# First stage of a hybrid HGRN2/Hyena layer: modulation and transposes before the filter kernels' blocks, all four v units in one stage, small tables on another queue

## The chip, the cores and the metric

The kernel runs on one core of one Trainium2 chip. A core has five engines with an instruction stream each, which they work off strictly in order: TensorE (PE, matmuls and transposes; its weight loads are listed as PEld), VectorE (DVE), ScalarE (ACT), GpSimd (POOL) and SyncE (SP, which here issues most transfers). An engine waits on semaphores of the others; work that stands behind a waiting instruction on the same engine waits with it. The metric is the device time of one execution in microseconds; less is better.

## The reference

One layer of a flow-matching backbone in float32: 128 context tokens and 512 sample tokens (T = 640) of width 1024. Cut to what matters for the change:

```python
# modulation of the tokens by a condition (context tokens by c_ctx, sample tokens by c)
mod = silu(c) @ ada_w + ada_b                 # six parts of 1024
h = x * (1 + scale) + shift                   # parts 0 and 1
z = h @ w_in                                  # 5 HGRN, 3 Hyena, 2 gate parts
# HGRN2, in both directions, 8 heads of 128
v = heads(i_raw)                              # a part of z
fg = lb + (1 - lb) * sigmoid(f_raw); k = 1 - fg
# chunks of 32 tokens, b = cumsum(log fg):
q_in = q * exp(b); k_in = k * exp(-b); k_st = k * exp(b_last - b)
# Hyena: filters from a small network
hf = sin(freq[0] * (z_pos @ w1 + b1))
hf = sin(freq[1] * (hf @ w2 + b2))
hf = sin(freq[2] * (hf @ w3 + b3))
filt = (hf @ w4) * window                     # then a long convolution through its spectrum
```

After both mixers come gates, an output projection, a layer norm, a SwiGLU feed-forward block and a second norm.

## The kernel before

Matrix products in float32 are made of three passes: each operand is split into a rounded high part and a low part (hi/lo, names with h and l), and high x high, high x low and low x high are summed. A split takes a cast (ScalarE or VectorE) and a subtraction (VectorE or POOL).

The kernel runs in stages: the first stage, up to 115.6 us of the profile; M1 (the large projections, a Winograd-like scheme); the Hyena convolution with its projection; HGRN; and the output and feed-forward stages. The changed parts lie in the first stage, and in HGRN's beginning. The first stage does:

- the filter network (L495 to L508): matmuls f1, f2 and f3, each followed by a sine layer of four VectorE operations (L479 to L483) and a Sin on ScalarE; its result is split into `hf_hi` and `hf_lo`;
- the tables `kt` (`ktab`, L512): three loads, each with a cast to `kth` and a difference `ktl` on POOL;
- the tokens `x`: five loads of 512 KB (`x_load`, L450), transposed by TensorE into `xT` (`x_transpose`, L457), ten groups of four transposes;
- the modulation: for each of four blocks `nb` of 512 columns two loads of 1 MB (`ada_load`, L397), eight matmuls in two quads (`ada_quad`, L406), a copy `md` on ScalarE (L417), four transposes `adaT` (L430) and additions on VectorE into `modT`. The loads' buffers are three (`araw`);
- `make_h` (L459 on), for each of eight blocks `k`: two modulation operations, a cast to `hTh` and a difference `hTl`. Tables of letters say which engine does which: `HMOD` for the modulation, `HSUB` for the difference (S ScalarE, V VectorE, G POOL);
- the filter kernels, for each of four channel blocks `cc`: `kern_load` (w4 and win), `kern_a` (the weights `wsd`, `whi`, `whl`; ten matmuls `ks`; five windows `af` with two buffers; their splits `abh` and `abl`), `kern_b` (6 matmuls `kp` and 48 matmuls `k`, then sums into `ko`) and a store to `kd`;
- v units (L696): a product of all tokens with 256 columns, 120 matmuls each, with weights that are loaded as `raw` and split into `wh` and `wl`. v0 and v1 are made here, v2 and v3 in the HGRN stage, after head 0's gate g0;
- the block operands of M1 (step `e`).

The order is a string of steps, `PLAN`, read from left to right: `x0` is a load, `T0` its transposes, `L0`, `A0`, `B0`, `W0` the parts of filter block 0, `k0` a table, `D0` the two loads of modulation block 0 and `M0` its quads, copy and transposes, `h0` a `make_h`, `V0` a v unit, `p`, `t`, `q` the parameters. The instructions of a step are handed to a scheduler, which keeps the order of each buffer and places work on each engine by dependency and by order in the string; `tc.high_priority()` moves work ahead. Steps such as `M0` and the splits of weights have that priority before the change. The HGRN stage has a string of its own, `HGSEQ`: for head 0 `a0 b0 q0 g0` are projections, `e0` the element chain of exponentials and products on ScalarE and VectorE (`t`, `ff`, `gg`, `xx`; `hg_elem`, L1157 on), and `s0` begins with TensorE's transposes `kT` (L1233) of one of its results, `t6`.

The stream of weights looks ahead by the table `LOOK`, and `HIE` and `WSUB` say by which engine each weight tile is cast and subtracted. Both are read by the tile's number.

Of the kernel before, what the change touches and what calls it, by code (L numbers as in the profile page):

```python
# [162 lines left out]
def body(tc, I, O):  # L163
# [16 lines left out]
    def tt(out, a, b, op, eng=None):  # L180
        return (eng or V).tensor_tensor(out=out, in0=a, in1=b, op=op)  # L181

# [123 lines left out]
    def params_T():  # L306
        ps = tr_bank("pr3_ps")
        PE.transpose(ps[:, 0:65], prow2, ident[0:65, 0:65])
        V.tensor_copy(cT.rearrange("p a k -> p (a k)"), ps[:, 49:65])
# [90 lines left out]
    def ada_quad(nb, i):  # L400
        raw = ada["raw"].pop((nb, i))
        if i == 0:
            ada["ps"][nb] = mm_bank(f"ada{nb}")
        ps = ada["ps"][nb]
        for g in range(4):
            PE.matmul(ps[32 * g:32 * g + 32, :], scT[:, 4 * i + g, :], raw[:, g, :], start=i == 0, stop=i == 1)  # L406
# [70 lines left out]
    def sin_layer(psrc, i, nm):  # L477
# [5 lines left out]
        V.tensor_scalar(a, a, HALF, -HALF, ALU.min, ALU.max)  # L483
        act(a, a, AF.Sin, scale=-TWO_PI)
# [7 lines left out]
    def filter_mlp():  # L492
# [10 lines left out]
        for hf in range(2):  # L503
            ps = sc_bank(f"f3_{hf}")
            rs = slice(hf * ORD, hf * ORD + ORD)
            PE.matmul(ps[:, 0:HT], w3[rs].rearrange("p a n -> p (a n)"), h2[rs], start=True, stop=True)
# [5 lines left out]
    def ktab(i):  # L512
# [3 lines left out]
        cpy("k", i, kth[:, cs], raw)  # L516
# [42 lines left out]
    def kern_b(cc, ab):  # L559
        c0 = cc * 256  # L560
        kth_ = (kth, ktl)
        def kout(n, nm):
# [4 lines left out]
            return t
# [6 lines left out]
        t = kout(1, "p")  # L574
        cpy("o", 3 * cc, t[:, 0], pk.rearrange("p (x n) -> p x n", x=2))
        out = [(t, 4, 1)]
        for kt in range(2):
# [12 lines left out]
            t = kout(2, kt)  # L590
# [8 lines left out]

    def order_after(ins, prev):  # L600
        if prev is not None:
            tc.add_manual_dep(
                ins.ins, prev.ins.name,
                mybir.DependencyInfo(mybir.DependencyClass.NoSync, mybir.DependencyReason.DATA),
                reason="issue order")
# [112 lines left out]
    v_add(0)  # L718
    v_add(1)
# [3 lines left out]
    def start():  # L723
        stream["stop"] = 4
# [1061 lines left out]
```

## Time and profile before

| quantity | value |
|---|---|
| runs | 1427.77, 1429.8 and 1691.48 us |
| median of the runs | 1429.8 us |
| the profiled execution's own time | 1430.8 us |
| its span on the core | 1428.1 us |

A row of the timeline has the start and the busy time in us, engine, line, operation, the tile written and those read, partitions x elements, a count (xcount) and in brackets the idle time of the engine before it with what ended it. The page's slices are tenths of busy time over 40 equal parts of the span of 35.7 us each; the first stage is the first three and a bit:

```profile
PE   4989999999999999999999999998999999999997
DVE  6886786647889734568778875578876766766427
ACT  3655554433323212455565673337444434442121
POOL 4230000020000000000000000000000000000003
DMA  7944665674333374422232224632343233357211
```

The waits of the queue that issues the loads, up to 110 us (waited for: us in total, times, longest):

```profile
SPq L526 <- DVE af L181: 18.3, 2, 9.2
SPq L450 <- PE xT L457: 6.1, 1, 6.1
SPq L397 <- PE ada L406: 4.6, 2, 2.5
```

A load of `win` waits until the windows before it are used up, a load of `x` or of the modulation until its buffer is free; all loads behind it in SP's queue wait with it.

### The profile page before, as it was taken

The numbers are of one execution on the slowest core, as the hardware profiler recorded it, in microseconds if no ns is written. First come the engines' busy times: TensorE is split into PE (matmuls) and PEld (weight loads), VectorE is DVE, ScalarE is ACT, GpSimd is POOL, SyncE is SP. The second block draws the span as 40 slices with busy tenths as digits, with TensorE's granted clock in tenths as the row PEclk, the third lists the DMA queues.
The fourth block names the chain that finished last, engine by engine and source line by source line (L and its number), as shares of the span: only waits on it lengthen the run. The fifth ranks groups of instructions, "written<-read, shape, count | busy, mean of one in ns | idle before, by whom it ended". The sixth has DMA issues, their size and how long they took to land. (4 is left out here: it accounts for less than half of the span.)

```text
span 1428.1 us, 23421 instructions
## 1 busy us (share of the span) xinstructions
PE 1377.5 (96%) x9513; PEld 1291.3 (90%) x9513; DVE 990.8 (69%) x1751; ACT 619.4 (43%) x1011; POOL 63.4 (4%) x56
## 2 busy tenths in 40 slices
PE   4989999999999999999999999998999999999997
PEld 2689889999999999999999999988999998998886
DVE  6886786647889734568778875578876766766427
ACT  3655554433323212455565673337444434442121
POOL 4230000020000000000000000000000000000003
PEclk9999999999999999999999999999999999999999
DMA  7944665674333374422232224632343233357211
GB/s 244 332 138 144 214 215 175 206 249 152 91 97 107 107 231 146 140 85 80 76 95 62 67 67 139 223 118 77 97 124 115 89 108 97 94 193 279 74 60 74
DMA packets 198855, 195.63 MB, mean 137 GB/s; under 512 B 7581, under 2 KB 155773, under 8 KB 197980
## 3 DMA queue, kind: packets, MB, share of 16 engines
q1 hardware_dynamic: 194860, 179.75, 40.0%
q0 software_dynamic: 2160, 9.15, 1.7%
q10 hardware_dynamic: 1728, 5.24, 0.9%
q8 instruction: 74, 1.21, 0.3%
q14 instruction: 33, 0.27, 0.1%
HBM read 162.91 MB, written 31.21 MB: 136 GB/s over the span
## 5 line engine op out<-in xcount | busy, mean ns | idle before, releaser
L181 DVE TENSOR_TENSOR wl<-raw,wh 128x1024 fp32r<-128x1024 f32 x96 | 117.2, 1223 | 134.1 <-ACT wh L357 133.4
L357 ACT CAST wh<-raw 128x1024 fp32r<-128x1024 f32 x90 | 94.1, 1049 | 221.1 <-PE pb L611 41.0
L1424 PE MATMUL fo<-wh,act 128*128 128x512 f32 (+1 forms) x440 | 130.6, 380 | 0.0
L1424 PEld LDWEIGHTS fo<-wh,act 128*128 128x128 f32 x440 | 81.2, 188 | 15.9
L1424 PE MATMUL fo<-wl,act 128*128 128x512 f32 (+1 forms) x220 | 83.4, 379 | 0.0
L611 PE MATMUL hy<-hTh,wh 128*128 128x320 f32 x256 | 79.6, 311 | 0.0
L611 PE MATMUL hy<-hTh,wl 128*128 128x320 f32 x256 | 79.1, 309 | 0.0
L611 PE MATMUL hy<-hTl,wh 128*128 128x320 f32 x256 | 79.1, 309 | 0.0
L611 PE MATMUL f<-hTh,wh 128*128 128x320 f32 x224 | 70.7, 316 | 0.0
L611 PE MATMUL f<-hTl,wh 128*128 128x320 f32 x224 | 69.6, 311 | 0.0
L611 PE MATMUL f<-hTh,wl 128*128 128x320 f32 x224 | 69.2, 309 | 0.0
L181 POOL TENSOR_TENSOR y<-y,gb 128x512 f32<-128x512 f32 x8 | 11.6, 1453 | 905.8 <-ACT y L170 905.5
L1424 PEld LDWEIGHTS fo<-wl,act 128*128 128x128 f32 x220 | 41.3, 188 | 7.9
L611 PEld LDWEIGHTS hy<-hTh,wh 128*128 128x128 f32 x256 | 48.1, 188 | 0.0
L611 PEld LDWEIGHTS hy<-hTl,wh 128*128 128x128 f32 x256 | 48.1, 188 | 0.0
L611 PEld LDWEIGHTS hy<-hTh,wl 128*128 128x128 f32 x256 | 48.0, 188 | 0.0
L170 ACT ACT_TABLE_LOAD x36 | 46.2, 1283 | 1.4 <-PEq L1770 0.7
L708 PE MATMUL v<-wh,hTl 128*128 128x256 f32 x160 | 45.1, 284 | 1.4 <-POOL hTl L181 1.4
L708 PE MATMUL v<-wl,hTh 128*128 128x256 f32 x160 | 44.8, 284 | 1.6 <-DVE wl L181 1.6
L708 PE MATMUL v<-wh,hTh 128*128 128x256 f32 x160 | 44.6, 283 | 0.0
L611 PEld LDWEIGHTS f<-hTl,wh 128*128 128x128 f32 x224 | 42.2, 188 | 0.0
L611 PEld LDWEIGHTS f<-hTh,wh 128*128 128x128 f32 x224 | 42.1, 188 | 0.0
(2291 smaller groups left out, 4699.1 us busy)
## 6 DMA issues: line engine op xcount, KB each, us to landing
raw<-in_w_in SPq DMA_DIRECT2D x52, 512.0 KB, 3.9
rf<-in_ffn_w_in SPq DMA_DIRECT2D x42, 512.0 KB, 4.9
araw<-in_ada_w SPq DMA_DIRECT2D x20, 1024.0 KB, 6.1
rm<-in_w_in SPq DMA_DIRECT2D x28, 512.0 KB, 4.8
raw<-in_ffn_w_out SPq DMA_DIRECT2D x22, 512.0 KB, 4.9
sd<-my SPq DMA_DIRECT2D x28, 320.0 KB, 2.3
kk<-kd SPq DMA_DIRECT2D x20, 256.0 KB, 2.6
ad<-y SPq DMA_DIRECT2D x16, 320.0 KB, 4.0
```

The lines of the kernel that those rows point to most:

```text
L170: r = S.activation(out, in_, func, bias=bias, scale=scale)
L181: return (eng or V).tensor_tensor(out=out, in0=a, in1=b, op=op)
L357: (V.tensor_copy if HIE[i] == "V" else S.copy)(hi, raw)
L611: r = PE.matmul(ps[:, 0:HT], w[a][:, k, :], x[b][:, k, c0:c0 + HT], start=k == 0 and i == 0, stop=k == kt - 1 and i == 2)
L708: PE.matmul(ps[:, (t - t0) * 256:(t - t0) * 256 + 256], hT[b][:, k, t * P:t * P + P], w[a][:, k % 4, :], start=k == 0 and i == 0, stop=k = ...
L1424: PE.matmul(ps, x(t, b, k0 + kk), w[a][:, kk, :], start=first and kk == 0 and i == 0, stop=last and kk == nk - 1 and i == 2)
```

## The change

`PLAN` is written anew up to M1's first steps, and some work changes its engine, buffer or queue. Before:

```text
x0 k0 L0 k1 x4 k2 p mlp t L1 T0 x3 T4 A0 x2 D0 T2 A1 x1 L2 B0 M0 T1 D2 A2 M2 T3 h0 L3 B1 D1 A3 h1 B2 M1 D3 h2 h3 M3 h4 W2 W0 h5 h6 h7 W1 q V0 e0 B3 g0 W3 V1 m w0 e2
```

After:

```text
x0 L0 x4 a0 a1 x3 c mlp k0 k1 k2 a4 p t T0 T4 T3 a5 x1 x2 M0 M1 Y0 A0 L1 M4 M5 Y2 T1 T2 a2 a3 h0 h1 h2 h3 B0 A1 L2 M2 M3 Y1 a6 a7 W0 M6 M7 Y3 h4 h5 h6 h7 B1 A2 L3 W1 B2 A3 W2 q B3 W3 e0 e2 V0 V1 V2 g0 V3 m w0
```

- Modulation goes in single steps, `a` (one load), `M` (one quad) and `Y` (copy, transposes, additions), with no priority. `a4 a5` are the two loads of block 2.
- All x is loaded and transposed, and blocks 0 and 2 of the modulation are made, before block 0's `kern_b`. M1's operands `e0 e2` come ahead of the v units.
- v2 and v3 leave `HGSEQ` and follow v1 in the first stage; all v tiles share one buffer. The tables `HIE` and `LOOK` are moved by four tiles to match.
- The modulation of `make_h` is all ScalarE's (k = 1 and 4 were VectorE's). The differences `wl` of weight tiles 1, 2, 5, 6 and 7 go from POOL to VectorE. All three `kth` casts are ScalarE's (one was VectorE's), and must follow the last sine of the network.
- `wsd` of block 0 must follow the last VectorE operation of the second sine layer, and the first modulation matmul must follow f3.
- The conditions c and c_ctx get a tile of their own, `crow`, with an own transpose, `cond_T`; they and the four loads of w2 and w3 are issued by ScalarE. The sigmoid of the condition thus runs ahead of the sines, with one more table load.
- The tiles `ko` use the buffers of `araw`, and `kop` those of `xs`.

The diff, cut to its core:

```diff
-HMOD = "SVSSVSSS"
+HMOD = "SSSSSSSS"
-WSUB = "VGGVVGGG"
+WSUB = "VVVVVVVVVVVV"
...
-HGSEQ = """a0 b0 q0 g0 e0 v2 v3 a1 b1 q1 g1 s0 e1 a2 b2 q2 g2 s1 e2 a3 b3 q3 g3 s2 e3 a4 b4 q4 g4 s3 e4 a5 b5 q5 g5 s4 e5 a6 b6 q6 g6 s5 e6 a7 b7 q7 g7 s6 e7 s7 c m0 m1 t m2 m3 p0 m4 p1 m5 p2 m6 p3 m7 p4 p5 p6 p7"""
+HGSEQ = """a0 b0 q0 g0 e0 a1 b1 q1 g1 s0 e1 a2 b2 q2 g2 s1 e2 a3 b3 q3 g3 s2 e3 a4 b4 q4 g4 s3 e4 a5 b5 q5 g5 s4 e5 a6 b6 q6 g6 s5 e6 a7 b7 q7 g7 s6 e7 s7 c m0 m1 t m2 m3 p0 m4 p1 m5 p2 m6 p3 m7 p4 p5 p6 p7"""
...
+    crow = sp.tile([16, P], F32, name="crow")
+    S.dma_start(crow[0:8], I["c_ctx"].rearrange("(k p) -> k p", p=P))
+    S.dma_start(crow[8:16], I["c"].rearrange("o (k p) -> (o k) p", p=P))
     for hf in range(2):
-        SY.dma_start(w2[hf * ORD:hf * ORD + ORD], I["filt_w2"][0])
+        S.dma_start(w2[hf * ORD:hf * ORD + ORD], I["filt_w2"][0])
     for hf in range(2):
-        SY.dma_start(w3[hf * ORD:hf * ORD + ORD],
-                     I["filt_w3"][0].unsqueeze(1).to_broadcast([ORD, 2, ORD]))
+        S.dma_start(w3[hf * ORD:hf * ORD + ORD],
+                    I["filt_w3"][0].unsqueeze(1).to_broadcast([ORD, 2, ORD]))
...
+    def cond_T():
+        ps = tr_bank("pr2_ps")
+        PE.transpose(ps[:, 0:16], crow, ident[0:16, 0:16])
+        V.tensor_copy(cT.rearrange("p a k -> p (a k)"), ps[:, 0:16])
         act(csig, cT, AF.Sigmoid)
...
-    def ada_mods(nb, q):
-        with tc.high_priority():
-            for i in range(2):
-                ada_quad(nb, i)
-            ada_vec(nb, q)
+            r = PE.matmul(ps[32 * g:32 * g + 32, :], scT[:, 4 * i + g, :], raw[:, g, :], start=i == 0, stop=i == 1)
+            if (nb, i, g) == (0, 0, 0):
+                order_after(r, net["f3"])
...
-        cpy("k", i, kth[:, cs], raw)
+        order_after(S.copy(kth[:, cs], raw), net["sin", "31"])
...
+        for i, op in enumerate((ALU.add, ALU.subtract)):
+            r = tt(wsd[:, i], w4[:, 0], w4[:, 1], op)
+            if cc == 0:
+                order_after(r, net["clamp", "2"])
...
+        ko = se.tile([P, 2, 2, 2, 256], F32, tag="araw", bufs=3, name=f"ko{cc}")
...
-            v = (vp if p < 2 else hg["p"]).tile([P, NB, 256], F32, tag="v", bufs=1 + p // 2, name=f"v{p}")
+            v = vp.tile([P, NB, 256], F32, tag="v", bufs=1, name=f"v{p}")
...
-        stream["stop"] = 4
+        stream["stop"] = 8
```

Three places of the order on the engines. In the rows a tile's name has its block's number (`ks0_1`: block 0, window 1) and ends in the buffer's number.

First, VectorE between the first and the second sine layer, before the change: the cast of the first table and the two differences of `wsd0` stand between the clamp of layer 1 (L483) and the first operation of layer 2 (L479).

```order
L483 TENSOR_SCALAR sa1_175<-sa1_175 128x320
L184 CAST kth_135<-kt0_141 128x768
L181 TENSOR_TENSOR wsd0_259<-w4_0_145 128x256 x2
L479 TENSOR_SCALAR sa2_185<-f2_182,fpar_103 128x320
L481 TENSOR_SCALAR sk2_187<-sa2_185 128x320
```

After the change, the same place:

```order
L492 TENSOR_SCALAR sa1_166<-sa1_166 128x320
L488 TENSOR_SCALAR sa2_176<-f2_173,fpar_106 128x320
L490 TENSOR_SCALAR sk2_178<-sa2_176 128x320
L491 SCALAR_TENSOR_TENSOR sa2_176<-sk2_178,sa2_176 128x320
L492 TENSOR_SCALAR sa2_176<-sa2_176 128x320
L181 TENSOR_TENSOR wsd0_303<-w4_0_144 128x256 x2
```

The cast has left VectorE, and `wsd0` stands behind the clamp of layer 2.

Second, SP's queue of loads, before: the tables `kt` are the first large loads beside `xs0`, and the modulation's loads (`araw`) come after four loads of x.

```order
L450 DMA xs0_139<-in_x_prompt 128x1024
L515 DMA kt0_141<-in_kt 128x768
L523 DMA w4_0_145<-in_filt_w4 64x2x256 x2
L526 DMA win0_148<-in_win 128x5x256
L515 DMA kt1_150<-in_kt 128x768
L450 DMA xs4_154<-in_x_sample 128x1024
L515 DMA kt2_156<-in_kt 128x768
L523 DMA w4_1_224<-in_filt_w4 64x2x256 x2
L526 DMA win1_227<-in_win 128x5x256
```

After:

```order
L459 DMA xs0_142<-in_x_prompt 128x1024
L532 DMA w4_0_144<-in_filt_w4 64x2x256 x2
L535 DMA win0_147<-in_win 128x5x256
L459 DMA xs4_149<-in_x_sample 128x1024
L410 DMA araw0_0_151<-in_ada_w 128x4x512
L410 DMA araw0_1_153<-in_ada_w 128x4x512
L459 DMA xs3_155<-in_x_sample 128x1024
L524 DMA kt0_206<-in_kt 128x768
L524 DMA kt1_210<-in_kt 128x768
L524 DMA kt2_214<-in_kt 128x768
L410 DMA araw2_0_218<-in_ada_w 128x4x512
L410 DMA araw2_1_277<-in_ada_w 128x4x512
```

The tables now stand behind two loads of 1 MB and one more load of x. On ScalarE the casts of the tables stand ahead of the casts `abh` of block 0, and `md2`, which TensorE's `adaT2` needs, behind all five of them; after the change:

```order
L525 CAST kth_138<-kt0_206 128x768
L191 COPY xT3_135<-xT3_1_270 128x2x128
L525 CAST kth_138<-kt1_210 128x768
L525 CAST kth_138<-kt2_214 128x768
L191 CAST abh0_0_318<-af0_0_314 128x512
L191 CAST abh0_1_329<-af0_1_325 128x512
L191 CAST abh0_2_338<-af0_2_336 128x512
L191 CAST abh0_3_347<-af0_3_345 128x512
L191 CAST abh0_4_356<-af0_4_354 128x512
L426 COPY md2_374<-ada2_365 128x512
```

Before, two of these casts stood ahead of the second and third sine, and the copies of `md` had no block of filter casts ahead of the first of them but block 0's own.

Third, TensorE in the HGRN stage, after the change: f1 of head 1, then three of the transposes of head 0's `t6`, then g1.

```order
L610 MATMUL f1_1_1_6552<-hTh3_626,wh36_6366 128x320
L610 MATMUL f1_1_1_6552<-hTl3_627,wh36_6366 128x320
L610 MATMUL f1_1_1_6552<-hTh3_626,wl36_6367 128x320
L1233 MATMUL kT0_0_6645<-cst_84,t6_0_6429 128x128 x3
L610 MATMUL g1_0_6587<-hTh0_417,wh37_6463 128x320
L610 MATMUL g1_0_6587<-hTl0_418,wh37_6463 128x320
```

Before the change all eight transposes stand behind g1, and v2's first rows directly behind g0:

```order
L611 MATMUL g0_1_6119<-hTh3_888,wh30_5919 128x320
L611 MATMUL g0_1_6119<-hTl3_889,wh30_5919 128x320
L611 MATMUL g0_1_6119<-hTh3_888,wl30_5920 128x320
L708 MATMUL v2_0_6189<-wh31_5987,hTh0_600 128x256
L708 MATMUL v2_0_6189<-wh31_5987,hTl0_601 128x256
```

With v2 and v3 gone from here, 96 matmuls (f0 and f1 of head 1) lie between g0's end and the first of `kT`, where before 240 matmuls of v2 and v3, these 96 and 48 of g1 did.

More of the change, by code (lines that the diff above doesn't have):

```diff
@@ L181, in tt, with order_after @@
         return (eng or V).tensor_tensor(out=out, in0=a, in1=b, op=op)
+    def order_after(ins, prev):
+        if prev is not None:
+            tc.add_manual_dep(
+                ins.ins, prev.ins.name,
+                mybir.DependencyInfo(mybir.DependencyClass.NoSync, mybir.DependencyReason.DATA),
+                reason="issue order")
     def cpy(which, i, out, in_):
@@ L304, in params_load @@
         G.dma_start(msk, I["msk"])
[L306 to L309, printed above, removed]
+    def cond_T():
+        ps = tr_bank("pr2_ps")
+        PE.transpose(ps[:, 0:16], crow, ident[0:16, 0:16])
+        V.tensor_copy(cT.rearrange("p a k -> p (a k)"), ps[:, 0:16])
         act(csig, cT, AF.Sigmoid)
@@ L312, in params_T @@
             tt(scT[:, :, a:a + 1].rearrange("p k a -> p a k"), cT[:, a:a + 1, :], csig[:, a:a + 1, :], ALU.mult)
+    def params_T():
+        ps = tr_bank("pr3_ps")
+        PE.transpose(ps[:, 0:49], prow2, ident[0:49, 0:49])
         V.tensor_copy(prT2, ps[:, 0:49])
@@ L393, in body @@
     ada = dict(raw={}, ps={})
+    net = {}
     def ada_load(nb, i, q, tag, bufs, eng=SY):
@@ L405, in ada_quad @@
         for g in range(4):
-            PE.matmul(ps[32 * g:32 * g + 32, :], scT[:, 4 * i + g, :], raw[:, g, :], start=i == 0, stop=i == 1)
-    def ada_mods(nb, q):
-        with tc.high_priority():
-            for i in range(2):
-                ada_quad(nb, i)
-            ada_vec(nb, q)
+            r = PE.matmul(ps[32 * g:32 * g + 32, :], scT[:, 4 * i + g, :], raw[:, g, :], start=i == 0, stop=i == 1)
+            if (nb, i, g) == (0, 0, 0):
+                order_after(r, net["f3"])
     def ada_vec(nb, q):
@@ L482, in sin_layer @@
         V.scalar_tensor_tensor(a, k, MAGIC, a, ALU.subtract, ALU.subtract)
-        V.tensor_scalar(a, a, HALF, -HALF, ALU.min, ALU.max)
-        act(a, a, AF.Sin, scale=-TWO_PI)
+        net["clamp", nm] = V.tensor_scalar(a, a, HALF, -HALF, ALU.min, ALU.max)
+        net["sin", nm] = act(a, a, AF.Sin, scale=-TWO_PI)
         return a
@@ L505, in filter_mlp @@
             rs = slice(hf * ORD, hf * ORD + ORD)
-            PE.matmul(ps[:, 0:HT], w3[rs].rearrange("p a n -> p (a n)"), h2[rs], start=True, stop=True)
+            net["f3"] = PE.matmul(ps[:, 0:HT], w3[rs].rearrange("p a n -> p (a n)"), h2[rs], start=True, stop=True)
             h3 = sin_layer(ps[:, 0:HT], 2, f"3{hf}")
@@ L573, in kern_b @@
                           start=i == 0, stop=i == 2)
-        t = kout(1, "p")
+        t = se.tile([P, 1, 2, 256], F32, tag="xs", bufs=3, name=f"kop{cc}")
         cpy("o", 3 * cc, t[:, 0], pk.rearrange("p (x n) -> p x n", x=2))
@@ L589, in kern_b @@
             od = pk[1].rearrange("p (x n) -> p x n", x=2)
-            t = kout(2, kt)
+            t = ko[:, kt]
             tt(t[:, 0], od, ev, ALU.add)
@@ L598, in kern_store @@
             KQ.dma_start(kd[cc, :, f:f + n], t)
[L600 to L605, printed above, removed]
     def dense_fm(w, x, half, ps, kt=KT, after=None):
@@ L716, in v_add @@
         U(v_unit(p), w_tm(w_in, 0, 4, COL_I + p * 256, 256), w_tm(w_in, 4, 4, COL_I + p * 256, 256))
-    v_add(0)
-    v_add(1)
+    for p in range(4):
+        v_add(p)
     vu = units[:]
@@ L741, in step @@
                 ktab(i)
-            elif op == "D":
-                for n in range(2):
-                    ada_load(i, n, se, "araw", 3)
+            elif op == "a":
+                ada_load(*divmod(i, 2), se, "araw", 3)
             elif op == "Q":
@@ L752, in step @@
             elif op == "M":
-                ada_mods(i, se)
+                ada_quad(*divmod(i, 2))
+            elif op == "Y":
+                ada_vec(i, se)
             elif op == "h":
@@ L764, in step @@
             else:
-                dict(p=params_load, t=params_T, q=params)[op]()
+                dict(p=params_load, c=cond_T, t=params_T, q=params)[op]()
         for tok in PLAN.split():
```

20 lines of the change are left out of this document (5 added, 15 removed).

## The prediction

> **What bounds the kernel now.** I read the page first, then the windows by stage, then the waits of the first stage, then single rows of the places that the change touches. On the page TensorE is the bound:
>
> ```profile
> PE 1377.5 (96%) x9513; PEld 1291.3 (90%) x9513; DVE 990.8 (69%) x1751; ACT 619.4 (43%) x1011; POOL 63.4 (4%) x56
> ```
>
> The span is 1428.1 us, so TensorE is idle for 50.6 us in all. The change leaves the matmuls as they are in number and shape, so it can win only from these 50.6 us and from matmuls that run on a slow clock. A measurement of this kernel tells about 2% from no change, 28.6 us; that is more than half of all the idle time. The windows (columns: window, length, busy of PE, PEld, DVE, ACT, POOL with counts, granted clock, DMA share, GB/s):
>
> ```profile
> 0.00:24.00 24.00, 7.83 (x33) 4.44 (x34) 12.40 (x36) 6.73 (x14) 13.61 (x22) 1.00 0.81 237
> 24.00:50.00 26.00, 22.58 (x128) 14.73 (x131) 23.38 (x47) 12.66 (x27) 7.01 (x5) 0.87 0.78 276
> 50.00:72.00 22.00, 20.94 (x151) 14.61 (x143) 18.68 (x44) 16.83 (x31) 6.43 (x6) 1.00 0.99 351
> 72.00:115.60 43.60, 39.73 (x325) 39.12 (x326) 38.32 (x58) 23.49 (x38) 12.04 (x6) 1.00 0.36 125
> 23.40:34.00 10.60, 8.18 (x28) 4.36 (x29) 10.23 (x21) 7.63 (x18) 1.36 (x1) 0.69 0.81 287
> ```
>
> The first stage, up to the first matmul of M1 at 115.6 us, has 115.6 - 91.1 = 24.5 us of TensorE's idle time, 16.2 of it before 24 us, and its clock is low only from 23.4 to 34 us. What ends these waits (total, times, longest):
>
> ```profile
> PE f L506 <- ACT sa L170: 7.3, 1, 7.3
> PE pr_ps L276 <- DMA frow<-in_filt_b: 4.6, 1, 4.6
> PE f L500 <- ACT sa L170: 2.5, 1, 2.5
> PE ks L543 <- ACT abh L184: 2.4, 1, 2.4
> PE k L585 <- DVE af L181: 2.1, 1, 2.1
> PE ks L543 <- ACT hf_hi L184: 1.8, 1, 1.8
> PE v L708 <- POOL hTl L181: 1.4, 2, 0.7
> PE v L708 <- DVE wl L181: 1.0, 1, 1.0
> DVE af L181 <- POOL abl L181: 5.7, 3, 3.5
> ```
>
> **The change part by part.**
>
> *The filter network's chain, -4.3 us.* Its longest wait, 7.3 us, is VectorE's order, not arithmetic:
>
> ```profile
> 8.55 1.33 PE L500 MATMUL f<-sa,w 64*64 64x320 f32 x4 [2.46 <-ACT sa L170]
> 10.41 0.56 DVE L184 CAST kth<-kt 128x768 fp32r<-128x768 f32 x1 [2.42 <-DMA kt<-in_kt]
> 12.91 0.76 DVE L181 TENSOR_TENSOR wsd<-w 128x256 f32<-128x256 f32 x2 [1.93 <-DMA w<-in_filt_w]
> 13.59 0.60 DVE L479 TENSOR_SCALAR sa<-f,fpar 128x320 f32<-128x320 f32 x1
> 17.21 1.44 PE L506 MATMUL f<-sa,w 64*128 64x320 f32 x4 [7.33 <-ACT sa L170]
> ```
>
> f2 is done at 8.55 + 1.33 = 9.9, yet its first VectorE operation stands behind a cast and a difference that wait for loads. The change moves both off that place. From 13.59 to 17.21 the chain takes 3.6 us, of which about 1.0 is two operations of whl between; without them 2.6. The new small transpose and its table load on ScalarE put f2 back by an estimated 0.4 us. So f3 begins near 9.9 + 0.4 + 2.6 = 12.9 instead of 17.21: -4.3, with ends of 0 (the loads of w2 and w3 come late from ScalarE's queue) and -4.7. The loads of the parameters that leave SP's and POOL's queue cost those nothing: SP's four issues take some 0.5 us each ahead of x0, whose data TensorE wants only after f3.
>
> *hf_hi, -1.3.* ks waits 1.8 us for the third sine. In the new order 16 transposes, two modulation quads, eight more transposes and adaT0 stand between f3 and ks0, about 8 us; I leave 0.5 us (ends -1.8 and +1).
>
> *ks1, -2.4 and +2.0.* ks1's wait of 2.4 us on abh goes, since ks1 now follows B0. In its place whl1 stands on ScalarE behind steps h0 to h3, now all of ScalarE:
>
> ```profile
> 54.12 1.22 ACT L170 ACTIVATE xT<-xT,modT 128x128 f32<-128x128 f32 x2
> 55.69 0.75 ACT L184 CAST hTh<-xT 128x640 fp32r<-128x640 f32 x1
> ```
>
> Four times 1.22 + 0.7 is 7.6 us, begun when the last xT copy is out, near 38; TensorE has 54 matmuls of B0 and one quad, 7.5 us from about 36, so it waits 2 us (ends 0 and 4).
>
> *The modulation's loads ahead of the work that needs them, +3.4.* ada2's two quads follow ks0 at once. By SP's order 6.7 MB are ahead of or in araw2_0 and 7.7 MB with araw2_1. The windows give 237 x 24 = 5.7 MB by 24 us; at the same pace up to 0.38 MB/us after it (rows below) they land at 26.6 and 29.3. The rows w4_1 and win1 (short packets) now come later, so I take 25.3 and 28.0. ks0 ends near 23.6, a quad takes 1: waits of 1.7 and 1.7 (ends 0 and 4.4).
>
> ```profile
> 24.00:26.00 2.00, 2.00 (x6) 1.11 (x6) 1.78 (x6) 1.99 (x5) 0.00 (x0) 0.50 1.01 377
> 26.00:28.00 2.00, 2.00 (x10) 1.60 (x10) 2.00 (x7) 1.15 (x3) 0.78 (x1) 0.65 1.04 392
> ```
>
> *A new in-order chain, +4.3.* kt's loads move behind ada0 and x3, its casts behind the last sine on ScalarE, and so POOL's three differences come late. Before, they were over at 21.9:
>
> ```profile
> 20.07 1.85 POOL L181 TENSOR_TENSOR ktl<-kt,kth 128x768 fp32r<-128x768 f32 x1 [1.37 <-ACT kth L184]
> 27.22 1.36 POOL L181 TENSOR_TENSOR abl<-af,abh 128x512 fp32r<-128x512 f32 x1 [5.30 <-ACT abh L184]
> 37.27 0.59 ACT L417 COPY md<-ada 128x512 f32<-128x512 f32 x1 [3.25 <-PE ada L406]
> 24.59 0.69 DVE L181 TENSOR_TENSOR af<-ks,win 128x512 f32<-128x512 f32 x1 [0.22 <-PE ks L544]
> ```
>
> POOL had 5.3 us of slack before abl0_0. Now kt0 lands near 21, its cast ends at 22.8, and three differences of 1.8 us end at 28.2; abl0_0 ends at 29.5; af0_2, which needs abl0_0's buffer, frees VectorE; af0_3 and af0_4 with two abl between take 5 x 0.65 to 32.9; abh0_4 and then md2 on ScalarE end at 33.7. TensorE, in order, has adaT2 ahead of three of xT1's transposes and stands from 29.4 to 33.7. Ends: 0 (kt lands at once) and 6.5 (at the slower pace above). The same pattern, VectorE behind POOL's abl, costs VectorE 5.7 us already before.
>
> *The clock, -1.0.* The slow stretch before cost about 0.31 x 8.18 = 2.5 us. After 12.9 us TensorE is busy in more of the time, but stands up to 7.7 of the 10 us behind 23.6; I take 1.5 us of loss (ends 0 and 4.2).
>
> By the Trainium skill, "TensorE: Matmul & The Clock Gate", Part 1, an idle window of about 3.4 us halves the clock until about 3.4 us of activity have passed. The trace agrees only in part: after the idle 7.33 us the granted clock is 1.00 up to 23.4 and falls to 0.50 at 24. By that rule the new gap of 4.3 us adds an estimated 1.7 us, and the sum below would be 2.8 instead of 1.1 (rival 5).
>
> *Blocks and v units, -1.4.* Late in the stage TensorE waits 2.1 (k on af), 1.4 (POOL's hTl) and 1.0 (wl) = 4.5 us. V0 now takes the place of waiting work, and wl moves from POOL to VectorE at 1.2 us each; but hTl3 still comes from POOL, near 70 us. I leave 3.1 (ends 1 and 6.5). ko's tiles in other buffers, the store's queue and the wider prefetch cost nothing: DMA is busy for a third of the time from 72 us on.
>
> *v2 and v3 move, -0.7 and +2.5.* Two units of 14.2 us go from the HGRN stage to the first stage unchanged, and their one wait there goes:
>
> ```profile
> 583.43 0.39 PE L708 MATMUL v<-wl,hTh 128*128 128x256 f32 x1 [0.68 <-DVE wl L181]
> 559.50:566.50 7.00, 7.00 (x49) 7.00 (x49) 4.25 (x12) 1.48 (x2) 0.00 (x0) 1.00 0.63 212
> 566.50:596.25 29.75, 29.07 (x243) 28.87 (x242) 18.86 (x26) 15.31 (x20) 0.00 (x0) 1.00 0.39 126
> 596.25:617.40 21.15, 21.15 (x147) 21.14 (x146) 5.21 (x5) 6.68 (x10) 0.00 (x0) 1.00 0.53 162
> ```
>
> But these 29.75 us covered head 0's element chain, which starts when g0 ends at 566.5:
>
> ```profile
> 574.37 3.60 ACT L170 ACTIVATE t<-t 128x1280 f32<-128x1280 f32 x3
> 581.02 0.82 DVE L181 TENSOR_TENSOR t<-t,gg 128x640 f32<-128x640 f32 x1
> 582.16 1.22 DVE L181 TENSOR_TENSOR wl<-raw,wh 128x1024 fp32r<-128x1024 f32 x1
> 617.37 1.04 PE L1233 MATMUL kT<-cst,t 128*128 128x128 f32 x8
> ```
>
> kT needs the row at 581.02, done at 581.8, 15.3 us after g0's end. After the change one wl (1.2 us) stands in that chain: 16.5. The order now has three of kT's transposes ahead of g1, so only f0 and f1 cover it, two thirds of 21.15 = 14.1. TensorE waits 2.4, with kT's own start 2.5 (ends 0, were the chain shorter by its ScalarE part, and 5, with a second wl in it).
>
> *Sum.* -4.3 - 1.3 - 2.4 + 2.0 + 3.4 + 4.3 - 1.0 - 1.4 - 0.7 + 2.5 = +1.1 us. The profiled execution took 1430.8 us, 2.7 outside its span, and stands 1.0 above the median of the runs, 1429.8. So 1431.9 against the profile, 1430.9 against the median: 1431.
>
> **The rivals.**
> 1. *Slower: POOL's queue.* kt lands at the slower pace (+2.2), the third difference ends near 30.5, and the clock halves in the gap (+2.7, the upper end above), so first-stage work runs behind and hTl3 with it (+3.4, the upper end): 1439. For it: SP's order. Against: POOL was 4% busy. It decides from abl0_0 starting after 30 us.
> 2. *Faster: the chain is covered.* kt lands by 20, abl0_0 starts by 26, adaT2 waits 0.3 (-4.0), araw2 lands in time (-3.4): 1424. For it: DMA moved up to 392 GB/s in a row above. Against: 16 queues are at a share of 1.0 there already.
> 3. *Hidden anyway.* f3 comes early, but ada0's data do not, and TensorE spends the 4.3 us waiting there: 1435. Against: 3.9 MB up to araw0_1 at 237 GB/s are in at 16.6.
> 4. *HGRN alone at its upper end* of 5 us: 1433.5. For it: the order puts kT ahead of g1. Against: only one wl is in the chain by the order.
> 5. *The gap halves the clock.* After a stand of 4 us the matmuls run once more as at 24 to 28 us, where granted 0.50 and 0.65 over 2 us each lost 1.0 + 0.7 = 1.7 us: 1433. For it: that stretch. Against: the clock stayed at 1.00 for 6 us after the longest idle time.
>
> **How the numbers follow.** My forecast, no change that can be told, near 1431 (1427 to 1436, its smaller errors): 0.44. Rival 1: 0.17; rival 2: 0.20; rival 3: 0.06; rival 4: 0.05; rival 5: 0.08. The range takes in rivals 2 to 5 and rival 1 to just above its time: 1421 to 1440; what is left out is a little of rivals 1 and 2. Faster by over 2% would need 28.6 us out of 50.6: 0.02. Slower by over 2% would need every upper end and as much again: 0.03. Within 2%: 0.95.
>
> **What would show it.** Right: f3 near 12.9; adaT2 starting some 4 us after ada2's end, with abl0_0 behind three ktl on POOL; M1's first matmul at 143 to 146 (115.6 + 29.8 = 145.4 is no change); one wait of 2 to 3 us at kT of head 0. Wrong: f3 near 17 again; no idle time between 23 and 34 us; M1 under 140 or over 150; any wait over 2 us in the later stages that before did not have.

## The result and the profile after

The changed kernel is slower by 0.6%: ratio of the times 1.0059, 95% interval 1.0043 to 1.0075, that is 6 to 11 us. The median of its five runs is 1436.7 us (1433.8 to 1438.0); the kernel before took 1427.8 us on the same chip (the median of five runs, of which one in the slow state, at 1691.5 us, is left out of the ratio). So it lies within 2% and in the range, but on the slow side of the forecast.

The page of the changed kernel (engine, busy time, share of the span of 1432.0 us, instructions; its profiled execution took 1433.8 us and is the fastest of the five):

```profile
PE 1380.8 (96%) x9514; PEld 1297.0 (91%) x9514; DVE 1000.8 (70%) x1751; ACT 623.1 (44%) x1016; POOL 49.9 (3%) x49
```

TensorE is idle for 1432.0 - 1380.8 = 51.2 us; before it was 50.6. Yet it is busy for 3.3 us longer with the same matmuls: what was lost is pace, not waiting. Where it was lost is read from the starts of the first matmul of each part:

| first matmul of | before, us | after, us | difference |
|---|---|---|---|
| M1 | 115.63 | 148.15 | 32.52, of which 29.75 are v2 and v3, moved here |
| g0 (HGRN, head 0) | 559.47 | 592.56 | 33.09 |
| kT of head 1 | 649.05 | 656.67 | 7.62 |
| the feed-forward part | 973.25 | 980.87 | 7.62 |

The first stage lost 32.52 - 29.75 = 2.8 us, and the way from M1 to g0 0.6. Between g0 and the second kT the difference falls by only 25.5 us, though v2 and v3, 29.75 us, left this stretch: 4.3 us are lost there. Nothing is lost between that kT and the feed-forward part. The feed-forward part runs the same code and took 3.7 us less in this one execution, so the two profiled executions differ by less than the medians do.

The windows of the first stage, with the columns as before:

```profile
0.00:24.00 24.00, 13.20 (x69) 7.74 (x69) 13.96 (x43) 11.75 (x25) 9.00 (x19) 1.00 0.88 301
24.00:50.00 26.00, 19.09 (x108) 13.72 (x109) 17.21 (x29) 14.43 (x28) 8.13 (x5) 0.74 0.85 266
72.00:100.00 28.00, 25.62 (x183) 24.16 (x183) 22.09 (x41) 12.08 (x22) 8.26 (x6) 0.94 0.31 116
34.00:36.00 2.00, 1.70 (x8) 1.70 (x9) 0.33 (x2) 0.25 (x1) 1.11 (x1) 0.50 1.04 380
38.00:40.00 2.00, 2.00 (x11) 2.00 (x11) 0.81 (x2) 1.79 (x6) 0.00 (x0) 0.50 1.10 261
76.00:80.00 4.00, 3.58 (x22) 3.38 (x21) 2.78 (x4) 1.75 (x3) 2.74 (x2) 0.72 0.33 129
```

Up to 24 us TensorE is busy for 13.2 us where it was 7.8: work did come earlier. But from 24 to 50 us the granted clock is 0.74 where it was 0.87, and it drops again near 76 to 80 us. Busy time times (1 - granted clock), summed over windows of 2 us up to M1, gives 5.9 us lost by a low clock, and 3.1 before. The idle time up to M1 is 24.75 us, and 24.53 before, with v2 and v3 now inside. So in this execution the stage won nothing in waits, and its loss is what the low clock took: 2.8 us by these windows, 2.5 if the ends of the record's half-clock stretches are taken.

That split belongs to this one execution. The profile of E4 below has the same order on TensorE up to M1. There M1 begins at 149.15, the idle time is 26.89 us and the windows give 4.5 us lost by the clock: 2.4 us more waiting than before the change and 1.4 of clock. The new waits are 0.8 us for whl and this one:

```profile
19.75 1.07 PE L419 MATMUL ada<-araw,scT 128*32 128x512 f32 x8 [1.60 <-DMA araw<-in_ada_w]
```

That the first stage is slower is seen in both; how much of it is clock is not settled.

TensorE's timeline (start, duration, instruction, in brackets the idle time before it and what ended it):

```profile
12.93 1.50 PE L515 MATMUL f<-sa,w 64*128 64x320 f32 x4 [2.49 <-ACT sa L170]
25.26 1.06 PE L419 MATMUL ada<-araw,scT 128*32 128x512 f32 x8 [1.76 <-DMA araw<-in_ada_w]
27.97 1.93 PE L419 MATMUL ada<-araw,scT 128*32 128x512 f32 x8 [1.65 <-DMA araw<-in_ada_w]
34.30 1.12 PE L439 MATMUL adaT<-cst,md 128*128 128x128 f32 x4 [4.00 <-ACT md L426]
35.21 3.41 PE L466 MATMUL xT<-cst,xs 128*128 128x128 f32 x15
38.27 0.56 PE L578 MATMUL kp<-abh,kth 128*128 128x256 f32 x1
162.70 0.41 PE L667 MATMUL ma<-m4h,wma0h 128*128 128x320 f32 x1 [1.41 <-ACT mu L676]
616.11 0.55 PE L1233 MATMUL kT<-cst,t 128*128 128x128 f32 x3 [2.26 <-DVE t L181]
```

f3 begins at 12.93; the loads of ada2 are waited for (1.76 and 1.65), adaT2 for 4.00, kT for 2.26. All four stand where the prediction put them. What it put too low is the loss of pace behind the waits: the second quad of ada2 takes 1.93 instead of 1.06, and 15 transposes take 3.41 us.

### The profile page after: what moved, and what is told of

Its sections match the earlier page's. It is cut to its first block, busy times and chain, and to the rows that moved or that the text cites. A ratio compares the mean times of both kernels' runs of the same rounds, so it can differ in the third digit from the quotient of the medians.

```text
span 1432.0 us, 23457 instructions
## 1 busy us (share of the span) xinstructions
PE 1380.8 (96%) x9514; PEld 1297.0 (91%) x9514; DVE 1000.8 (70%) x1751; ACT 623.1 (44%) x1016; POOL 49.9 (3%) x49
## 5 line engine op out<-in xcount | busy, mean ns | idle before, releaser
L181 DVE TENSOR_TENSOR wl<-raw,wh 128x1024 fp32r<-128x1024 f32 x101 | 123.2, 1222 | 113.7 <-ACT wh L369 112.7
```

## The experiments

The experiments were timed against the kernel before on their own chips. A and B are theories of the 4.0-us wait at adaT2: A, POOL's queue delays abl0_0, as predicted; B, VectorE itself is slow beside POOL's three differences ktl. C is a theory of the whole loss: the half clock after a wait costs time of its own.

**E1: block 0's first filter difference, abl0_0, off POOL.**

```
-ASUB = "GVVVGVGVGGGGVGVGVVVG"
+ASUB = "VVVVGVGVGGGGVGVGVVVG"
```

> The changed kernel with one difference abl0_0 on VectorE instead of POOL; TensorE's, ScalarE's and all other orders are the same. In the trace of the changed kernel adaT2 starts at 34.30 us after 4.00 us of waiting. Theory A (POOL's queue: abl0_0 stands behind three ktl and VectorE waits for its buffer): adaT2 starts near 31, its wait is under 1.5 us, the time falls by 3 to 4 us. Theory B (VectorE is never idle from 21.7 to 33.7 us; its one-row additions beside POOL's ktl take 1.3 to 1.9 us instead of 0.4): VectorE gets 0.7 us more to do, adaT2 starts at 34.3 to 35.0, the time does not fall.

Measured: 1.0058 (1.0046 to 1.0070), as without the edit. TensorE's row in E1:

```profile
35.53 1.12 PE L439 MATMUL adaT<-cst,md 128*128 128x128 f32 x4 [4.43 <-ACT md L426]
```

abl0_0 no longer stands in POOL's queue, and the wait is as long as ever: from the second quad of ada2 to adaT2 it takes 6.45 us, and 6.33 without the edit (all of it starts 1.1 us later, as the loads came later). So A falls. Why is seen on VectorE in the changed kernel:

```profile
21.69 0.69 DVE L181 TENSOR_TENSOR af<-ks,win 128x512 f32<-128x512 f32 x1
...
22.41 1.81 DVE L181 TENSOR_TENSOR af<-af 1x256 f32<-1x256 f32 x1
...
24.26 1.93 DVE L561 SCALAR_TENSOR_TENSOR af<-af,skp_all 1x256 f32<-1x256 f32 x1
26.12 0.67 DVE L181 TENSOR_TENSOR af<-ks,win 128x512 f32<-128x512 f32 x1
26.82 1.31 DVE L181 TENSOR_TENSOR af<-af 1x256 f32<-1x256 f32 x1
28.17 1.38 DVE L561 SCALAR_TENSOR_TENSOR af<-af,skp_all 1x256 f32<-1x256 f32 x1
...
50.63 0.41 DVE L181 TENSOR_TENSOR af<-af 1x256 f32<-1x256 f32 x1
```

and on POOL:

```profile
22.09 5.76 POOL L181 TENSOR_TENSOR ktl<-kt,kth 128x768 fp32r<-128x768 f32 x3 [13.66 <-ACT kth L525]
27.82 1.46 POOL L181 TENSOR_TENSOR abl<-af,abh 128x512 fp32r<-128x512 f32 x1
```

An operation on one row of 256 takes 0.41 us with POOL still, and 1.3 to 1.9 while POOL works. The four lose 4.8 us against 0.41 each, and VectorE has no gap of note from 21.69 to 33.7. They are held more than slowed: they end at 24.22, 26.19, 28.13 and 29.55, each 0.27 to 0.28 us after one of POOL's four operations ends (23.95, 25.91, 27.86 and 29.28). The multiplication by the window at 26.12, which reads one input from TensorE's output bank, takes its usual 0.67 us. The Trainium skill, "GPSIMD Engine Reference", section 1 "Specifications", says that GpSimd shares its SBUF interfaces with VectorE, with contention for DVE instructions that have two SBUF inputs. The trace agrees, and these rows give the size.

**E2: ktl on VectorE.**

```
-KSUB = "GGG"
+KSUB = "VVV"
```

> The changed kernel with the three differences ktl on VectorE instead of POOL; TensorE's order is the same, md2 comes one cast earlier on ScalarE. Theory B: the three cost VectorE 3 x 0.93 us, but the four one-row operations fall from 6.4 to 1.6 us, so adaT2 starts near 31.2 instead of 34.3, and the time falls by 2 to 5 us, the clock's part included. Theory A expects the same direction, 3 to 4 us. If neither holds (the wait is hidden behind ScalarE's h0 to h3 ahead of whl1), adaT2 comes early but ks1 still starts at 47.7 and the time stays within 1 us.

Measured: 1.0032 (1.0020 to 1.0044). VectorE has three differences more, and the one-row operations take 0.40 to 0.41. TensorE in E2:

```profile
32.72 1.11 PE L439 MATMUL adaT<-cst,md 128*128 128x128 f32 x4 [1.38 <-ACT md L426]
```

From the second quad of ada2 to adaT2 it takes 3.73 us instead of 6.33. It does so in every profile of this order without idle matmuls: 6.33 to 6.45 us in the four with ktl on POOL (the changed kernel, E1, E4, E6), 3.73 to 3.75 in the three with ktl on VectorE (E2, E7, A1). B stands. A wait of 0.24 us for whl now stands at ks1, the one that the prediction had as its +2.0.

**E3 and E5: idle matmuls in the waits.** The identity times itself, into a bank that nobody reads, n times ahead of the waiting matmul: in E3 12, 28 and 16 ahead of ada2's quads, adaT2 and kT, in E5 6, 14 and 9.

```
+    def warm(ps, n, prev):
+        for _ in range(n):
+            r = PE.matmul(ps[:, 0:P], ident, ident, start=True, stop=True)
+            order_after(r, prev)
+            prev = r
```

> The changed kernel with idle matmuls put into its waits: 12 ahead of each quad of ada2, 28 ahead of adaT2, 16 ahead of head 0's kT, each 128x128 into a bank that nobody reads; nothing is left out. The waits stay, TensorE is busy in them. Theory (the half clock that follows a wait costs time of its own): the granted clock stays near 1.00 from 24 to 40 us (0.50 and 0.65 in the changed kernel) and after kT (0.63); kT's part falls by 1.7 to 2.0 us; of the first stage's 3 to 4 us only about 1.1 arrive, since ks1 then waits for ScalarE. Total 3 us less than the changed kernel. Rival 1 (all of the lost clock is on the path): 6 to 7 us less. Rival 2 (the clock does not matter, the engines behind set the pace): within 0.7 us.

E3 measured 1.0109 (1.0096 to 1.0122), where 3 us less than the changed kernel had been expected. One such matmul took about 0.24 us, so the groups at ada2 and adaT2 outlasted the waits that they were to fill (adaT2 began at 37.79). The group for kT came to stand behind g1, as kT did, where TensorE waited for nothing, and added 3.6 us; and M1 to g0 grew by 3 us. Of the time E3 tells nothing. The granted clock was 1.00 from 20 to 50 us.

> As the run before with idle matmuls in the waits, but half as many, since each took 0.23 us and not 0.13: 6 ahead of each quad of ada2, 14 ahead of adaT2, 9 ahead of head 0's kT (all kT behind g1 or not, as the scheduler has it). They should end inside the waits, which keep their length. Theory (the half clock costs time of its own): granted clock 1.00 from 24 to 40 us, B0 done near 43.5 instead of 45.7; ScalarE's h0 to h3 then hold ks1, so M1 comes 1 to 2.5 us earlier than in the changed kernel's like runs (149.2); HGRN part 1.7 us shorter. Total 3 us less than the changed kernel, ratio to before near 1.004. Rival (the clock is not on the path): ratio 1.006.

E5 measured 1.0052 (1.0038 to 1.0065), not told apart from the change; 1.004 had been expected. Up to 36 us the clock did as expected; a window of E5:

```profile
24.00:36.00 12.00, 10.37 (x77) 7.75 (x76) 11.54 (x15) 4.99 (x9) 7.25 (x4) 1.00 1.07 333
```

and TensorE's timeline there:

```profile
36.93 0.66 PE L455 MATMUL adaT<-cst,md 128*128 128x128 f32 x4 [1.55 <-ACT md L440]
37.42 1.91 PE L484 MATMUL xT<-cst,xs 128*128 128x128 f32 x16
39.09 0.36 PE L598 MATMUL kp<-abh,kth 128*128 128x256 f32 x1
```

The stretch from adaT2 to kp0 takes 39.09 - 36.93 = 2.16 us; in the changed kernel it took 38.27 - 34.30 = 3.97 (one transpose less is in it). So the slow clock stretches this work by 1.8 us. In the time it does not show. Loads came late in E5 (ks0 2.5 us later). The half clock came later too: E5 has 0.66 from 56 to 66 us, where the changed kernel has 1.00, and its loss up to M1 is 4.6 us against 5.9. And the idle matmuls meant for kT ran behind g1, as in E3, 18 rows of them:

```profile
627.07 2.17 PE L415 MATMUL warmh<-cst 128*128 128x128 f32 x18
```

They delay kT to 629.08, by 2.0 us, and fill no wait. E5 also has kT behind g1, so in the HGRN stage it is not a test of the clock alone.

**E4: kT of head 0 behind g1.**

```
-                dense_fm(w, hT, half, ps)
+                hg["mm", which, h] = dense_fm(w, hT, half, ps)
...
-                PE.transpose(ps[:, i * P:i * P + P], k128[:, d, b * P:b * P + P], ident)
+                r = PE.transpose(ps[:, i * P:i * P + P], k128[:, d, b * P:b * P + P], ident)
+                if h == 0:
+                    order_after(r, hg["mm", "g", 1])
```

> The changed kernel with the transposes kT of head 0 tied behind g1's last matmul, where they stood before the change. Theory (the 2.26 us of waiting at kT and the half clock behind it, 0.63 and 0.94 over 7.9 us, cost 4.2 us): no wait at kT of head 0, granted clock 1.00 behind it, 4.2 us less. Rival 1 (only the wait counts): 2.3 us less. Rival 2 (the wait moves to the products behind kT): within 0.7 us.

Measured: 1.0034 (1.0022 to 1.0046). From g0 to the second kT it takes 61.36 us instead of 64.11. Expected had been 4.2 us less. The wait at kT is gone, but g1 now waits 1.26 us for its bank, which a sigmoid on ScalarE has to free. Windows of the changed kernel around kT:

```profile
599.60:616.10 16.50, 14.24 (x98) 13.98 (x96) 14.45 (x19) 13.37 (x17) 0.00 (x0) 1.00 0.58 197
616.10:620.00 3.90, 3.90 (x19) 3.90 (x20) 3.90 (x7) 0.88 (x3) 0.00 (x0) 0.63 0.02 5
```

a window of E4 there:

```profile
616.00:620.00 4.00, 3.21 (x22) 3.21 (x23) 4.00 (x7) 2.36 (x5) 0.00 (x0) 1.00 0.27 83
```

and on TensorE in E4 the row of the new wait:

```profile
616.79 0.41 PE L610 MATMUL g<-hTh,wh 128*128 128x320 f32 x1 [1.26 <-ACT sg L170]
```

A wait of 2.26 us is followed by 3.9 us at 0.63 (and 4.0 more at 0.94): 3.9 x 0.37 + 4.0 x 0.06 = 1.7 us lost. The wait of 1.26 us is followed by the full clock. One microsecond less of waiting gave 2.75. The record of the clock has half speed from 617.10 to 620.51 in the changed kernel, and a stretch of the same 3.41 us in E1 and E2, which wait 2.27 us here. It has none in A1, E3 and E5, whose wait at g1 is 1.26 or 1.27.

**A1: E2 and E4 together.** Both edits above, nothing else.

> The changed kernel with both repairs: the three ktl on VectorE, and head 0's kT behind g1. Each alone took 3.6 to 3.9 us off the changed kernel's ratio of 1.0059. If they are apart, the sum: ratio 1.0005 to 1.0015, M1 near 146.5, no half clock behind kT. If the late stages give part of it back, 1.002 to 1.003.

Measured: 1.0016 (1.0007 to 1.0025); the feed-forward part begins at 975.30, 2.1 us behind the kernel before instead of 7.6. The two repairs nearly add: 2.7 and 2.5 thousandths alone, 4.3 together. Of the 2.1 us that stay, 0.6 are there at M1 (146.02 against 115.63 + 29.75) and 1.5 lie between g0 and the second kT, where g1's wait is.

**E6 and E7: v2 and v3 back in the HGRN stage**, with the new first stage kept; E7 has E2's edit as well.

```
-PLAN = "... V0 V1 V2 g0 V3 m w0 ..."
+PLAN = "... V0 V1 g0 m w0 ..."
...
-HGSEQ = "a0 b0 q0 g0 e0 a1 b1 q1 g1 ..."
+HGSEQ = "a0 b0 q0 g0 e0 v2 v3 a1 b1 q1 g1 ..."
...
-        stream["stop"] = 8
+        stream["stop"] = 4
```

> The changed kernel with v2 and v3 back in the HGRN stage (their order, tiles and tables of numbers as before the change). Theory: from g0 to kT of head 1 the kernel is as before the change, 4.3 us less than in the changed kernel once the two units are taken off, no wait at kT, clock 1.00; the first stage is as in the changed kernel up to V1. Ratio to before near 1.003. Rival 1 (v2 and v3 are cheaper in the first stage, and M1's two waits of 1.4 us come with them or go): 0 to 2 us less than the changed kernel. Rival 2: with the first stage shorter, M1's operands come late and the gain is lost there.

E6 measured 1.0082 (1.0069 to 1.0095), where 1.003 had been expected. From g0 to the feed-forward part it takes 413.82 us, before the change 413.78: the loss in the HGRN stage does come from the move. But M1, at 119.58, waits at once. TensorE in E6:

```profile
128.84 0.63 PE L667 MATMUL mc<-m5h,wmu0h 128*128 128x320 f32 x1 [4.99 <-ACT wmu0h L618]
```

and from M1 to g0 it takes 450.4 us instead of 443.8: with the new first stage M1's weights come late, and v2 and v3 had covered that (the second rival of the expectation).

> Both: v2 and v3 back in the HGRN stage and the differences ktl on VectorE. If the two costs are apart, the gains add: 2.7 to 3.9 and 4.3 us, ratio to before 1.000 to 1.002. If the late start of the first stage hides one behind the other, the ratio stays at 1.003.

E7 measured 1.0045 (1.0033 to 1.0057): M1 is 1.5 us earlier than in E6, the wait of 5 us stays, so neither of the two expected ratios came out.

**B1: the filter chain's ties alone, in the kernel before.**

```
-PLAN = "x0 k0 L0 k1 x4 k2 p mlp t L1 ..."
+PLAN = "x0 L0 x4 p mlp k0 k1 k2 t L1 ..."
...
-        cpy("k", i, kth[:, cs], raw)
+        order_after(S.copy(kth[:, cs], raw), net["sin", "31"])
...
+            if cc == 0:
+                order_after(r, net["clamp", "2"])
```

> The kernel before with the ties of the filter network alone: wsd of block 0 behind the second clamp, the casts of kt on ScalarE behind the last sine, kt's loads behind x0, w4, win and x4; all else as before the change. Theory (the tie is worth 4.3 us at f3, and most of it arrives while no new wait follows): f3 near 12.9, ks0 near 19.5, M1 2 to 4 us earlier than 115.6, ratio 0.997 to 0.999. Rival 1 (hidden anyway: TensorE then waits for ada0's loads and ScalarE): f3 early, M1 within 1 us, ratio 1.000. Rival 2 (the ktl beside VectorE's one-row additions and a half clock eat it up, as in the changed kernel): M1 1 us later or more, ratio 1.001 or above.

Measured: 1.0014 (1.0004 to 1.0023). f3 begins at 12.53 instead of 17.21, and nothing of it is left: M1 begins at 116.42, 0.8 us later than before. TensorE in B1:

```profile
24.14 0.72 PE L554 MATMUL ks<-whl,hf_lo 128*128 128x512 f32 x2 [3.78 <-DVE hf_lo L181]
31.71 0.77 PE L553 MATMUL ks<-whl,hf_hi 128*128 128x512 f32 x1 [4.43 <-DVE whl L181]
```

and VectorE in B1, shortly before the first of them:

```profile
21.02 1.05 DVE L181 TENSOR_TENSOR wsd<-w 128x256 f32<-128x256 f32 x1 [1.50 <-DMA w<-in_filt_w]
21.99 2.09 DVE L181 TENSOR_TENSOR hf_lo<-sa,hf_hi 64x320 fp32r<-64x320 f32 x1
```

hf_lo stands behind block 1's wsd, which waits for its load, and then takes 2.09 us beside POOL's ktl instead of 0.48. The wait of 7.3 us has become two of 3.8 and 4.4.

**B3, B2, B4: the rest of the ties.** B3 puts block 1's wsd behind hf_lo; B2 is B3 with ktl on VectorE; B4 is B2 with idle matmuls, 8 ahead of x2's transposes and 3 ahead of each quad of ada0.

```
-            if cc == 0:
-                order_after(r, net["clamp", "2"])
+            if cc < 2:
+                order_after(r, net["clamp", "2"] if cc == 0 else net["lo"])
...
-KSUB = "GGG"
+KSUB = "VVV"
...
+        if nb == 0:
+            last = warm(3, net["pe"])
...
+            last = warm(8, net["ks"]) if (t, q) == (2, 0) else None
```

> The kernel before with the ties of the filter network and one more: wsd of block 1, which waits for its load, behind hf_lo. In the run with the ties alone ks0 began at 18.56 but stood 3.78 us for hf_lo, behind that wsd and stretched to 2.09 us beside POOL's ktl, and ks1 stood 4.43 us for whl. Theory (VectorE's order again): the wait of 3.8 us falls to 1.5 or less (the stretch stays), ks1 begins 1 to 2 us before 31.7, M1 1 us before 116.4: ratio 1.0005. Rival (ks1 waits for w4_1's data and ScalarE anyway): M1 within 0.5 us of 116.4, ratio 1.0014.

> The same with the three ktl on VectorE, so that POOL does nothing beside the first af. Theory (POOL beside VectorE's one-row and two-input work is the cost): hf_lo takes 0.5 us, no wait over 1 us inside ks0, ks1 begins near 28, M1 near 113, ratio 0.998. Rival (three ktl of 0.9 us on VectorE's path cost what the stretching cost): M1 within 1 us of 115.6, ratio 1.000 to 1.001.

Measured: B3 1.0005 and B2 1.0005 (both 0.9996 to 1.0014). In B3 the wait for hf_lo is gone; a wait of 3.7 us for a load of x and one of 4.0 for whl stand in its place, and M1 begins at 116.10, 0.5 later than before. B2, expected at 0.998, has 3.9 us less idle time up to M1 than the kernel before (20.7 against 24.5) and loses 2.4 us more by the clock (5.5 against 3.1); M1 begins at 115.45, 0.2 us earlier.

> The run with both ties and ktl on VectorE, and idle matmuls in three of its waits: 8 ahead of x2's transposes (it waited 2.54 us there), 3 ahead of each quad of ada0 (1.02 and 1.18 us); TensorE's order is the same around them, nothing is left out. That run had 20.7 us of idle time to M1 where the kernel before has 24.6, and M1 came only 0.2 us earlier; its clock was 0.50 from 26 to 36 us. Theory (the half clock gave the gain back): granted clock near 1.00 from 24 to 36 us, ks1 takes 0.23 us for a matmul instead of 0.43, kp of block 0 begins 1.5 to 2.5 us before 37.19, M1 1 to 2.5 us before 115.45: ratio 0.9985 to 0.9995. Rival 1 (transfers and VectorE set the pace behind kp, the clock hides): kp early, M1 within 0.7 us, ratio 1.0005. Rival 2 (idle matmuls do not hold the clock): clock as before, all as before.

Measured: 0.9976 (0.9965 to 0.9987), 1426.8 us against 1430.0: a little faster than both kernels, and by more than expected. A window of B2, its granted clock third from the end, and of B4:

```profile
24.00:36.00 12.00, 8.46 (x33) 4.18 (x34) 9.13 (x18) 5.27 (x11) 2.55 (x2) 0.57 0.88 295
```

```profile
24.00:36.00 12.00, 7.45 (x50) 4.94 (x51) 9.12 (x16) 5.17 (x11) 2.57 (x2) 1.00 0.84 285
```

TensorE's timeline over the same work (second matmul of a window of ks1, first of kp), in B2:

```profile
33.52 0.63 PE L554 MATMUL ks<-whl,hf_lo 128*128 128x512 f32 x1
37.19 0.28 PE L582 MATMUL kp<-abh,kth 128*128 128x256 f32 x1
```

and in B4:

```profile
33.59 0.39 PE L573 MATMUL ks<-whl,hf_lo 128*128 128x512 f32 x1
36.11 0.28 PE L603 MATMUL kp<-abh,kth 128*128 128x256 f32 x1
```

The clock is 1.00 instead of 0.57, and from 33.5 on the same work takes 2.52 us instead of 3.67. In these two executions M1 comes only 0.7 us earlier in B4, since its loads landed later; the runs differ by about 2.9 thousandths, 4 us, on two chips. That the whole difference is the clock is therefore not shown. That idle matmuls hold the clock is: in all eleven profiles without them the record halves for the first time between 24.0 and 33.6 us, and in the three with them (E3, E5, B4) not before 57 us.

## Why the prediction was right in the waits and wrong in the clock

The forecast was no change, +1.1 us; up to the feed-forward part the trace shows +7.6. Of the prediction's signs, f3, the wait at adaT2 and the one at kT came as named; M1, at 148.15, lies outside the 143 to 146 that were to show it right.

- *The filter network's chain, -4.3:* right. f3 at 12.93 against a forecast of 12.9; f2 came 0.57 later for an estimated 0.4, though the table loads are 36 before and after and not one more. B1 shows what it is worth alone: nothing, since the next in-order waits and late loads take it back.
- *The modulation's loads, +3.4:* right, 1.76 + 1.65 = 3.41.
- *A new in-order chain, +4.3:* right in size, 4.00, and wrong in mechanism. The prediction had POOL's queue and abl0_0's buffer behind it, and even its times for abl0_0 came out (28.2 forecast, 27.82 measured). E1 took abl0_0 from that queue and the wait stayed; E2 took POOL's work away and 2.6 us of the 6.33 went. VectorE, held up by POOL's differences of the same time, was the chain; the buffer came free just when VectorE was.
- *ks1, +2.0:* the wait for whl is not in this profile; several waits of 0.7 to 1.0 us near 52 to 60 us are there instead (in E1, E2, E4 and A1 whl is waited for, 0.2 to 0.8 us). Together with hf_hi and the blocks and v units the small terms even out: all forecast waits up to M1 came to -0.4 against before, with v2's 0.68 counted in, and the idle times above, 24.75 - (24.53 + 0.68), give -0.5. That the sum came out so well is in part luck, since E4's 26.89 would give +1.7.
- *v2 and v3 move, +2.5:* the wait was 2.26; from g0 to the second kT the stage lost 4.3. The clock behind the wait, 1.7, was left out. E4 and E6 show the place and the cause.
- *The clock, -1.0:* this is the step that failed. The prediction reasoned that TensorE is busy in more of the time and that before the clock had stayed high after the wait of 7.3 us, and lowered its loss from 2.5 to 1.5, with 4.2 as its upper end. It rose to 5.9, and 1.7 came in the HGRN stage: 5.5 us of the 6.5 by which the sum missed, in the place of -1.0 a +2.8 and a +1.7. In E4's profile the first-stage part is +1.4 and waits make up the rest; the 1.7 is the same wherever kT is waited for. The rest is 0.6 between M1 and g0, two waits of 1.4 us at 162.70 and 201.72 where there were smaller ones, and 0.4 that no row names.

So rival 5, the halved clock, is what happened, only in two places and, in this profile, at three times its price of 1.7. The reason against it, that the clock had stayed at 1.00 for 6 us after the longest idle time, was a misreading. The trace's record of the clock begins at 20.58 us in the kernel before, and the windows read 1.00 where there is no record. The transposes there ran slowly:

```profile
18.74 2.82 PE L457 MATMUL xT<-cst,xs 128*128 128x128 f32 x16
```

Sixteen transposes take 1.91 us at the full clock (last section). Here their starts are 0.21 us apart up to 20.45 and 0.11 apart from 20.63 on: the clock was low behind the wait of 7.3 us. The other rows that should have warned were there too: before, the clock was at 0.50 and 0.65 from 24 to 28 us, straight behind a stretch in which TensorE was idle for two thirds of the time. The change leaves that stretch nearly half idle (13.2 of 24 us busy) and sets waits of 1.8, 1.7 and 4.0 us right behind it. By the Trainium skill, "TensorE: Matmul & The Clock Gate", Part 1, the clock halves after an idle window of about 3.4 us that runs freely. The trace agrees that it halves, and its half-clock stretches ahead of the kernel's end last 3.41 us or a multiple of that (13.65 us from 26.59 on in the changed kernel), but the wait of 2.26 us was enough here, so a wait shorter than the page's window does not make it safe. What rival 3 had in mind, the gain on the filter chain given back at the next wait, is what B1 shows, only at hf_lo and whl and not at ada0's loads.

## What to carry to other kernels

A wait on TensorE costs its length and can cost slow matmuls behind it, so of two orders with the same idle time the one with shorter waits can win, and a few idle matmuls in a wait that cannot be removed may pay if they do not outlast it. When a wait is removed from an engine's order, look at the next load or operation in that order before counting the gain: here 4.7 us of it came back at once. To see whether an engine waits or is slowed, compare the duration of the same small operation with and without its neighbour, since a busy engine shows no wait. And before a term is read from one profile, look at another execution of the same order: here the share of the clock in the first stage was 2.8 us in one and 1.4 in the other.

## What had not been expected of the hardware

- VectorE's operations with both inputs in the core's memory take three to nearly five times as long beside POOL's differences: 1.3 to 1.9 us instead of 0.41 for one row of 256, 2.09 instead of 0.48 for 64x320. In the changed kernel they end 0.27 to 0.28 us after POOL's operation.
- Half a clock followed the wait of 2.26 us at kT in all three profiles that have it, and the wait of 1.26 at g1 in none of four. A wait does not always bring it: in E1 the clock stayed at 1.00 from 24 to 32 us through waits of 1.75 and 1.63 at ada2, behind which the changed kernel has 0.50.
- Transposes by matmul follow the granted clock too: 16 in 1.91 us at 1.00, 15 in 3.41 at 0.50.
- The granted clock reads 1.00 early in a run although the pace is slow. Its record begins at 20.58 us before the change, at 16.35 after it and at 22.32 in B2. TensorE in B2, where starts are 0.43 us apart for ks that run 0.24 apart later:

```profile
20.76 0.63 PE L554 MATMUL ks<-whl,hf_lo 128*128 128x512 f32 x1
21.18 0.63 PE L553 MATMUL ks<-whl,hf_hi 128*128 128x512 f32 x1
...
36.26 0.40 PE L553 MATMUL ks<-whl,hf_hi 128*128 128x512 f32 x1
36.50 0.39 PE L554 MATMUL ks<-whl,hf_lo 128*128 128x512 f32 x1
```

So ahead of the record's begin the spacing of equal matmuls tells the pace, and a loss summed from the record is too small. By an estimate, half of TensorE's busy time up to that point, 3.1 us are missing before the change, 3.2 after it and 5.9 in B2: the comparison of the two kernels stands, and B2's loss by the clock is larger than its 5.5.
